# The first modulation of a two-layer diffusion trunk: sixteen weight blocks split over TensorE, VectorE and GpSimd, or all on TensorE with 128-column passes

## The chip, the cores and the metric

One core of one Trainium2 chip. The metric is device microseconds (us) of one execution of the whole kernel, which is one launch. The median of three runs of the kernel before is 2028.92 us (2028.03 to 2032.21).

## The reference, cut to what matters

Two layers of a transformer trunk over 512 latent tokens and 256 context tokens of width 1024. Each layer begins with a modulated RMS norm, followed by one wide input projection:

```python
silu_c = jax.nn.silu(c)          # latent condition, (1, 1024)
silu_cc = jax.nn.silu(c_ctx)     # context condition, (1024,)
for l in range(DEPTH):
    mod = silu_c @ w_mod[l] + b_mod[l]       # 6 * 1024 columns
    mod_c = silu_cc @ w_mod[l] + b_mod[l]
    sh1, sc1, g1, sh2, sc2, g2 = jnp.split(mod[:, None, :], 6, axis=-1)
    csh1, csc1, cg1, csh2, csc2, cg2 = jnp.split(mod_c, 6)
    h = rms_norm(x, norm1[l]) * (1 + sc1) + sh1
    hc = rms_norm(ctx, norm1[l]) * (1 + csc1) + csh1
    ... = jnp.split(h @ w_in[l], IN_SPLITS, axis=-1)
    # two attention branches, gates, output projection, SwiGLU
```

The "first modulation" is the part of this that must be done before anything else in layer 0 can be: the shift `sh1` and the scale `sc1` for both conditions. They take 2048 columns of `w_mod[0]`, which are 16 blocks of 128 columns (8 of shift, numbers 0 to 7, and 8 of scale, numbers 8 to 15), each 128 x 1024 in f32 and 512 KB.

## The kernel before, in words

Channels lie on partitions: x is eight tiles of 128 channels by 768 tokens (512 latent, 256 context), numbered k = 0 to 7. A product with a weight is done in three passes of reduced f32 (`fp32r`): both operands are split into a high and a low half (`h` and `hl` of the activations, `wh` and `wl` of a weight), and high by high, high by low and low by high are summed in PSUM.

`start` (L532 on) is the opening of the program, until the first three projections `gk`, `gv` and `gq` stand in PSUM. Its steps, with the names that the profile uses:

- `token` (L565) loads an x tile; `square` (L569, ACT) and `total` (L573, DVE) sum the squares; `means` (L576, tile `st`, PE) averages over channels; `eps` and `power` (POOL) form the inverse root; `widen` (L591, tile `rb`, PE) spreads it over the partitions; `normed` (L599, DVE) multiplies each x tile by it.
- The modulation of one block n. There are three ways, picked by a letter in the table `FIRST`. **p**: `product` (L606) does eight matmuls on PE with the weight block as the stationary operand and the two columns of `ccol` (the two conditions) as the moving one; the result is 128 x 2. **d**: `reduced` (L613) multiplies and sums on DVE twice, once for each condition, along the rows of a transposed block (`wmodT`). **g**: the latent condition on DVE in this way, the context condition by a multiply on POOL (`times`, L617) and a sum on ACT (`summed`, L620). The ways d and g need the conditions as rows on all partitions (`crow`), made by 16 matmuls (`spread`, L549) and four copies (`unspread`, L557). Five blocks go by p, three by d, eight by g.
- `settle` (L623, DVE) adds the bias, and for a scale block multiplies by the norm's gain (tiles `mod` and `A`).
- `modulate` (L632) applies scale and shift to x tile k: it needs blocks k and 8 + k. Then `high` (L640, ACT) and `low` (L644, POOL or DVE) make `h` and `hl`. The strings `HOWU` and `HOWL` say which engine modulates and which makes the low half, tile by tile.
- `wraw`, `whigh`, `wlow` load and split the three projection weights (`wr`, `wh`, `wl`).
- `multiply` (L664, tile `pj`) does the three passes for projection i, token group s (512 latent, then 256 context) and tile k, and `evac` hands a finished PSUM tile to the next stage.

The order on every engine in this opening is set by `Ops.run` (L275): a list scheduler with a fixed cost for each step, which writes out one order for all engines. `FIRST` is the order of the loads on the SP queue ("x" an x tile, "w" a projection weight, a number a block). Into the gaps that the scheduler foresees on PE it puts `idle` matmuls (L723), 128 x 128 products with the identity whose result nobody reads, at a density of `WARM` = 0.8. Buffers of loaded blocks are reused: the load of a block waits for the users of the block five before it.

Everything behind the opening is scheduled by the same code in both kernels.

Of the kernel before, what the change touches and what calls it, by code (L numbers as in the profile page):

```python
# [12 lines left out]
F32 = mybir.dt.float32  # L13
F32R = mybir.dt.float32r
AF = mybir.ActivationFunctionType
ALU = mybir.AluOpType
# [4 lines left out]
P = 128  # L21
D = 1024
KB = D // P
# [21 lines left out]
for _n in ORDER:  # L45
    for _j in range(COLS[_n][1]):
# [28 lines left out]
]  # L75


FIRST = "x x x x 10p x x x x 0g 8d 1g 13p w 9p w 2p 11g 12p 3d w 4g 5g 6g 14d 7d 15g"

HOWU, HOWL, HOWW = "aaavaaav", "ggvggvgv", "ggv"  # L80
START, HOP, LAND = 4.06, 0.15, 0.25
SAME = dict(v=0.22, a=0.0, g=0.0, p=0.0)
WARM = 0.8
PROD = 2.5


RATE = dict(a=(0.06, 0.00083, "a"), e=(0.28, 0.00083, "a"), v=(0.065, 0.00105, "v"), w=(0.065, 0.00058, "v"),
            g=(0.07, 0.00218, "g"), p=(0.0, 0.19, "g"))
# [175 lines left out]
class Ops:  # L264
# [60 lines left out]
class Trunk:  # L325
# [206 lines left out]
    def start(self, h, pool, others):  # L532


        nc, d = self.nc, self.d
        mod = self.mod[0]
        spans = ((0, S), (S, T))
        nt = T // P
        row = lambda n, count: [pool.tile([P, D], F32, tag="row", name=self.name(n)) for _ in range(count)]
        crow, junk = row("crow", 2), row("junk", 3)  # L540
# [8 lines left out]
        def spread(i):  # L549
            cp = tiles["cp", i] = self.ps("n", "cp")  # L550
            for j in range(4):
                c = 2 * (4 * (i % 2) + j) + i // 2
                nc.tensor.matmul(
                    cp[:, j * P : (j + 1) * P], self.ccol[:, c : c + 1].to_broadcast([P, P]), self.ident,
                    start=True, stop=True)

        def unspread(i):  # L557
            half = i % 2
            nc.scalar.activation(crow[i // 2][:, half * 512 : half * 512 + 512], tiles["cp", i], AF.Copy)

        rows = []
        for i in range(4):
            rows.append(add("a", 0.48, unspread, (i,), [add("p", (1.71, 1.71, 0.87, 0.87)[i], spread, (i,), [], 0)], 0))

        def token(k):  # L565
            x.append(self.slot("x"))
# [36 lines left out]
        def fetch(n, src):  # L603
            raws[n] = self.raw(src, pool=pool)

        def product(n, i):  # L606
            m = self.bank(tiles, i)[:, 2 * n : 2 * n + 2]
            for j in range(KB):
                nc.tensor.matmul(
                    m, raws[n][:, j * P : (j + 1) * P], self.ccol[:, 2 * j : 2 * j + 2],  # L610
                    start=(j == 0), stop=(j == KB - 1), skip_group_check=True)

        def reduced(n, s):  # L613
            nc.vector.tensor_tensor_reduce(
                junk[0], raws[n], crow[s], 1.0, 0.0, ALU.mult, ALU.add, mod[:, s, n : n + 1])

        def times(n, to):  # L617
            nc.gpsimd.tensor_tensor(to, raws[n], crow[1], op=ALU.mult)

        def summed(n, to):  # L620
            nc.scalar.activation(to, to, AF.Copy, accum_out=mod[:, 1, n : n + 1])

        def settle(n, i):  # L623
            m = mod[:, :, n] if i is None else self.bank(tiles, i)[:, 2 * n : 2 * n + 2]
            if n < KB:
                nc.vector.tensor_scalar(mod[:, :, n], m, more[:, n : n + 1], None, op0=ALU.add)
            else:
                k = n - KB
                nc.vector.tensor_scalar(
                    self.A[0][0][:, :, k], m, more[:, n : n + 1], self.norms[:, 0, k : k + 1], op0=ALU.add, op1=ALU.mult)  # L630
# [7 lines left out]
                nc.vector.tensor_scalar(u, u, scale, shift, op0=ALU.mult, op1=ALU.add)  # L638

        def high(k):  # L640
            h[0].append(self.slot("h", F32R))
            nc.scalar.activation(h[0][k], x[k], AF.Copy)

        def low(k, eng):  # L644
            h[1].append(self.slot("hl", F32R))
            (nc.gpsimd if eng == "g" else nc.vector).tensor_tensor(
                h[1][k], x[k], h[0][k][:].bitcast(F32), op=ALU.subtract)

# [24 lines left out]
        def evac(i):  # L673
            reach(others[i])

        loaded, got, free, wdone, sums = [], {}, [], [], []
        products = 0
        last = None
        for what in FIRST.split():
            if what == "x":  # L680
                k = len(loaded)
                loaded.append(add("d", 1.09, token, (k,), [], 1))
                sq = add("a", 0.74, square, (k,), [loaded[k]], 1)
                last = add("v", 0.87, total, (k,), [last, sq], 1) if k else sq
                if k < KB - 1:
                    continue
                last = add("v", 0.08, eps, (), [add("p", 1.28, means, (), [last], 0)], 0)
                early = [
                    add("p", c, widen, (s,), [add("g", g, power, (s,), [last], 0)], 0)
                    for s, c, g in ((0, 0.86, 0.96), (1, 0.43, 0.63))]  # L690
                ready = [
                    [add("v", c, normed, (k, s), [early[s], loaded[k]], 2) for s, c in ((0, 0.6), (1, 0.33))]
                    for k in range(KB)]
            elif what == "w":
                i = len(wdone)
                hi = add("a", 0.95, whigh, (i,), [add("d", 1.45, wraw, (i,), [], 1)], 3)
                eng = HOWW[i]
                wdone.append((hi, add(eng, 2.31 if eng == "g" else 1.13, wlow, (i, eng), [hi], 3)))
            else:
                n, how = int(what[:-1]), what[-1]  # L700
                src = d["wmod0"][products] if how == "p" else d["wmodT"][n]
                at = add("d", 1.45, fetch, (n, src), free[-5] if len(free) >= 5 else [], 1)
                which = None
                if how == "p":
                    which = products
                    products += 1
                    users = ends = [add("p", PROD, product, (n, which), [at], 3)]
                else:
                    users = [add("v", 1.14, reduced, (n, s), [at] + rows, 3) for s in range(1 + (how == "d"))]
                    ends = users  # L710
                    if how == "g":
                        to = junk[1 + len(sums) % 2]
                        users = users + [add("g", 2.31, times, (n, to), [at] + rows + sums[-2:-1], 3)]
                        sums.append(add("a", 1.04, summed, (n, to), users[-1:], 3))
                        ends = ends + sums[-1:]
                free.append(users)
                got[n] = add("v", 0.16, settle, (n, which), ends, 1)
# [1070 lines left out]
    def run(self):  # L1788
        nc, tc, d = self.nc, self.tc, self.d
        joint = [(0, S), (S, T)]  # L1790
        self.flow = None
        with (
# [9 lines left out]
            h = ([], [])  # L1802
            with (
                tc.tile_pool(name="ps0n", bufs=1, space=PSUM, reuse_waits="tile") as psn,
                tc.tile_pool(name="ps0", bufs=1, space=PSUM, reuse_waits="tile") as psa,
                tc.tile_pool(name="n0", bufs=1, reuse_waits="tile") as pool_,
            ):
                self.psum = dict(n=psn, a=psa)
                pool = _Bufs(pool_, dict(rs=1, row=5, more=1, wr=5), dict(qt=self.spool))
                self.constants(cpool)  # L1810
                at = Front()
                spare = _Bufs(None, {}, dict(qt=self.spool))
                todo = self.prologue(0, h, joint, spare, at)
                self.start(h, pool, todo)
            xd = [self.dpool.tile([P, S], F32, name=f"xd{k}") for k in range(KB)]
            for l in range(DEPTH):
# [3 lines left out]
                n = spans[-1][1]  # L1820
# [3 lines left out]
                with (  # L1824
# [7 lines left out]
                    if not last:  # L1832
                        crow = self.conditions(stack.enter_context(
                            tc.tile_pool(name=f"c{l}", bufs=1, reuse_waits="tile")))
                        one = lambda l, n: lambda: self.mod_one(l, n, crow)
                        beside = [one(0, n) for n in range(16, 44)]
                    with tc.tile_pool(name=f"m{l}", bufs=1, reuse_waits="tile") as pool_:
                        pool = _Bufs(pool_, dict(rs=2, qt=5), slots)
# [4 lines left out]
                        x = []  # L1843
# [22 lines left out]
                    h = ([], [])  # L1866
# [27 lines left out]
                    if not last:  # L1894
                        at = Front()
# [126 lines left out]
def _layout(a):  # L2022

    c = np.ascontiguousarray
# [4 lines left out]
    def blocks(m):  # L2029

        k, n = m.shape
        return m.reshape(k // P, P, n // P, P).transpose(2, 1, 0, 3).reshape(n // P, P, k)

    win = []
    for l in range(DEPTH):
# [18 lines left out]
        wmod0=blocks(wm[0][:, : 2 * D])[[int(w[:-1]) for w in FIRST.split() if w[-1] == "p"]],  # L2054
# [26 lines left out]
```

## Time and profile before

| | |
|---|---|
| median of three runs | 2028.92 us (2028.03 to 2032.21) |
| the profiled execution | 2031.42 us, of which the profile's span is 2029.6 us |
| mean granted TensorE clock | 0.977 |
| PE busy in the span | 1954.4 us (96%) |
| DVE, ACT, POOL busy | 1373.0, 884.9, 532.4 us |
| last matmul of the opening (L671) starts | 84.29 us |

The profile shows one execution. A row of the timeline gives a start, a duration, an engine, the line, the operation, and output and inputs by name. A plain f32 matmul leaves two rows on PE, and two rows of weight load on PEld; an `fp32r` matmul leaves one of each. A table of windows gives for each stretch, after its start and end, its length, then the busy time and number of rows of each engine, the clock granted to TensorE as a share of full speed, the busy share of the DMA engines, and GB/s. Matmuls are pipelined, so the distance between starts, and not the duration of one row, is what a matmul costs in a stream.

### The profile page before, as it was taken

How to read it: one execution, taken by the hardware profiler on the slowest of the kernel's cores; microseconds unless marked ns; L12 is line 12 of the kernel's file. 1: busy time of each engine (PE TensorE's matmuls, PEld its weight loads, DVE VectorE, ACT ScalarE, POOL GpSimd, SP SyncE). 2: the span in 40 equal slices, each digit the busy share in tenths (PEclk: the TensorE clock that was granted, in tenths of full speed). 3: DMA queues.
4: the chain of work that ended last, by engine and by line, in shares of the span. 5: the costliest groups of instructions: out<-in, count | busy, mean ns of one | idle time of the engine just before them, and what ended most of it. 6: DMA issues, size and time to landing. Idle time of an engine off the chain costs nothing. (4 is left out here: it accounts for less than half of the span.)

```text
span 2029.6 us, 29667 instructions
## 1 busy us (share of the span) xinstructions
PE 1954.4 (96%) x11468; PEld 1767.9 (87%) x11468; DVE 1373.0 (68%) x2470; ACT 884.9 (44%) x1640; POOL 532.4 (26%) x273
## 2 busy tenths in 40 slices
PE   7999999989999999999999979999999989999998
PEld 6888999977899999999899868889988988888887
DVE  7577888766987999888857576888643563232326
ACT  4466666542235543333424245666543442222224
POOL 6522222234300000000000134332345124435444
PEclk7899999989999999999999989999999989999999
DMA  7211122134563134456321322112223632323233
GB/s 285 70 56 42 37 60 79 58 117 133 182 240 123 60 123 142 144 177 215 118 73 52 103 95 63 51 52 63 76 86 112 197 95 87 113 82 112 75 122 94
DMA packets 74364, 216.50 MB, mean 107 GB/s; under 512 B 8560, under 2 KB 12784, under 8 KB 74224
## 3 DMA queue, kind: packets, MB, share of 16 engines
q1 hardware_dynamic: 74224, 214.61, 33.0%
q8 instruction: 90, 1.47, 0.3%
q14 instruction: 50, 0.41, 0.1%
HBM read 202.52 MB, written 6.82 MB: 103 GB/s over the span
## 5 line engine op out<-in xcount | busy, mean ns | idle before, releaser
L359 POOL TENSOR_TENSOR wl<-wr,wh 128x1024 fp32r<-128x1024 f32 (+2 forms) x177 | 388.6, 2200 | 1159.7 <-ACT wh L357 1152.5
L357 ACT ACTIVATE wh<-wr 128x1024 fp32r<-128x1024 f32 (+2 forms) x253 | 231.7, 917 | 568.4 <-issue 188.8
L372 PE MATMUL pj<-h,wh 128*128 128x512 f32 (+1 forms) x720 | 265.3, 372 | 8.5 <-ACT wh L357 4.4
L372 PE MATMUL pj<-hl,wh 128*128 128x512 f32 (+1 forms) x720 | 257.4, 358 | 3.1 <-DVE hl L528 3.1
L372 PE MATMUL pj<-h,wl 128*128 128x512 f32 (+1 forms) x720 | 256.5, 357 | 0.6 <-POOL wl L359 0.5
L372 PE MATMUL po<-ph,wh 128*128 128x512 f32 (+1 forms) x560 | 192.6, 345 | 0.0
L372 PE MATMUL po<-pl,wh 128*128 128x512 f32 (+1 forms) x560 | 192.5, 345 | 0.0
L372 PE MATMUL po<-ph,wl 128*128 128x512 f32 (+1 forms) x560 | 191.3, 345 | 0.0
L1577 PE MATMUL qu<-r,w 128*128 128x384 f32 x960 | 177.3, 337 | 5.7 <-ACT tt L1584 3.1
L1444 DVE SCALAR_TENSOR_TENSOR x<-po,G,x 128x256 f32<-128x256 f32 (+3 forms) x176 | 101.2, 589 | 120.5 <-PE po L372 120.3
L1577 PEld LDWEIGHTS qu<-r,w 128*128 128x128 f32 x960 | 167.5, 189 | 9.4 <-ACT tt L1584 6.2
L372 PEld LDWEIGHTS pj<-h,wh 128*128 128x128 f32 x720 | 139.4, 194 | 25.1 <-ACT wh L357 4.9
L372 PEld LDWEIGHTS pj<-h,wl 128*128 128x128 f32 x720 | 138.9, 193 | 21.0 <-POOL wl L359 1.5
L372 PEld LDWEIGHTS pj<-hl,wh 128*128 128x128 f32 x720 | 139.8, 194 | 19.2 <-DVE hl L528 4.0
L372 PE MATMUL pf<-hl,wh 128*128 128x512 f32 (+1 forms) x384 | 144.0, 375 | 2.2 <-DVE hl L528 2.1
L372 PE MATMUL pf<-h,wh 128*128 128x512 f32 (+1 forms) x384 | 144.0, 375 | 0.9 <-ACT h L527 0.9
L372 PE MATMUL pf<-h,wl 128*128 128x512 f32 (+1 forms) x384 | 143.4, 373 | 0.0
L1004 ACT ACTIVATE pth<-tp 128x512 fp32r<-128x512 f32 x176 | 103.5, 595 | 67.5 <-PE tp L1054 37.5
L1005 DVE TENSOR_TENSOR ptl<-tp,pth 128x512 fp32r<-128x512 f32 x176 | 119.7, 685 | 14.9 <-ACT pth L1004 13.2
L1469 ACT ACTIVATE w<-wr 128x512 fp32r<-128x512 f32 x120 | 73.7, 628 | 103.3 <-PE qv L1577 22.1
L372 PEld LDWEIGHTS po<-pl,wh 128*128 128x128 f32 x560 | 105.6, 189 | 13.2
L372 PEld LDWEIGHTS po<-ph,wl 128*128 128x128 f32 x560 | 104.9, 188 | 13.7
(243 smaller groups left out, 4436.6 us busy)
## 6 DMA issues: line engine op xcount, KB each, us to landing
wr<-wmodT SPq DMA_DIRECT2D x91, 512.0 KB, 3.8
wr<-wfi SPq DMA_DIRECT2D x88, 512.0 KB, 3.5
wr<-win SPq DMA_DIRECT2D x68, 512.0 KB, 3.5
wr<-wo SPq DMA_DIRECT2D x32, 512.0 KB, 4.1
wr<-wfo SPq DMA_DIRECT2D x40, 256.0 KB, 2.7
wr<-wfo SPq DMA_DIRECT2D x24, 384.0 KB, 3.0
wr<-wp SPq DMA_DIRECT2D x32, 256.0 KB, 3.1
x<-x SPq DMA_DIRECT2D x16, 384.0 KB, 7.7
```

Source lines behind the costliest of these rows:

```text
L357: nc.scalar.activation(hi, raw, AF.Copy)
L359: (eng or nc.gpsimd).tensor_tensor(lo, raw, hi[:].bitcast(F32), op=ALU.subtract)
L372: nc.tensor.matmul(ps[:, : b - a], u[:, c], v[k][:, a:b], start=(k == 0 and i == 0), stop=(k == nk - 1 and i == 2),)
L1004: nc.scalar.activation(hi, tp, AF.Copy)
L1005: nc.vector.tensor_tensor(lo, tp, hi[:].bitcast(F32), op=ALU.subtract)
L1444: self.nc.vector.scalar_tensor_tensor(x[j][:, f:u], ps[:, f - a : u - a], self.G[l][i][:, s, j : j + 1], x[j][:, f:u], op0=ALU.mult, op1=A ...
L1469: nc.scalar.activation(t[:, :n], src, AF.Copy)
L1577: nc.tensor.matmul(banks[bank], u[:, c], v, start=(first and k == 0 and i == 0), stop=(k == kn - 1 and i == 2), skip_group_check=True)
```

## The change

The ways d and g go, with `crow`, `spread`, `unspread`, `reduced`, `times` and `summed`. All sixteen blocks go through `product`, and each of its eight matmuls has 128 moving columns now instead of two: the same two columns of `ccol` repeated 64 times by a stride of zero. All 128 output columns of a block lie side by side in a PSUM bank; `settle` reads the first two. Two PSUM banks (`mp`) are used in turn, four blocks to a bank, before as after. A new constant `AHEAD` = 10 gives ten buffers of blocks instead of five (the five row buffers go), `FIRST` has another order of loads, `HOWU` and `HOWL` alternate the engines, the scheduler's cost of a product is 1.8 instead of 2.5, and the 16 tiles of h and hl are taken at the start of the opening.

```diff
-FIRST = "x x x x 10p x x x x 0g 8d 1g 13p w 9p w 2p 11g 12p 3d w 4g 5g 6g 14d 7d 15g"
-HOWU, HOWL, HOWW = "aaavaaav", "ggvggvgv", "ggv"
+FIRST = "8 x x 0 x x 9 x x 1 x x 10 2 w 11 3 w 12 4 w 13 5 14 6 15 7"
+AHEAD = 10
+HOWU, HOWL, HOWW = "avavavav", "gvgvgvgv", "ggv"
...
-PROD = 2.5
+PROD = 1.8
...
+        for k in range(KB):
+            h[0].append(self.slot("h", F32R))
+            h[1].append(self.slot("hl", F32R))
...
+        def moved(i):
+            return self.bank(tiles, i)[:, i // 2 % 4 * P : i // 2 % 4 * P + P]
+
         def product(n, i):
-            m = self.bank(tiles, i)[:, 2 * n : 2 * n + 2]
             for j in range(KB):
                 nc.tensor.matmul(
-                    m, raws[n][:, j * P : (j + 1) * P], self.ccol[:, 2 * j : 2 * j + 2],
+                    moved(i).rearrange("p (a b) -> p a b", b=2), raws[n][:, j * P : (j + 1) * P],
+                    self.ccol[:, 2 * j : 2 * j + 2].unsqueeze(1).to_broadcast([P, P // 2, 2]),
                     start=(j == 0), stop=(j == KB - 1), skip_group_check=True)
...
         def settle(n, i):
-            m = mod[:, :, n] if i is None else self.bank(tiles, i)[:, 2 * n : 2 * n + 2]
+            m = moved(i)[:, 0:2]
...
-                n, how = int(what[:-1]), what[-1]
...
+                n, i = int(what), len(free)
+                at = add("d", 1.45, fetch, (n, d["wmod0"][i]), free[-AHEAD] if i >= AHEAD else [], 1)
+                free.append([add("p", PROD, product, (n, i), [at], 3)])
+                got[n] = add("v", 0.16, settle, (n, i), free[-1], 1)
...
-                pool = _Bufs(pool_, dict(rs=1, row=5, more=1, wr=5), dict(qt=self.spool))
+                pool = _Bufs(pool_, dict(rs=1, more=1, wr=AHEAD), dict(qt=self.spool))
```

The lines of the changed file are numbered differently: `product` is L598, `means` L565, `widen` L581, `settle` L606 and L609, `modulate` on DVE L618, `high` L621, `low` L624, `wlow` L639, `multiply` L649 and `idle` L686.

On PE, the part of the opening between the average over channels (`st`) and the first passes of the projections (`pj`) reads so in the kernel before, where the projections' passes stand between the products (`mp`):

```order
L579 MATMUL st_226<-ones,sq_140 128x1 x6
L723 MATMUL idle_122<-ident_sb 128x128 x8
L595 MATMUL rb_253<-ident_sb,rs_243 128x128 x4
L595 MATMUL rb_262<-ident_sb,rs_243 128x128 x2
L609 MATMUL mp_177<-ccol_sb,wr_241 128x2 x8
L609 MATMUL mp_176<-ccol_sb,wr_275 128x2 x8
L609 MATMUL mp_177<-ccol_sb,wr_302 128x2 x8
L671 MATMUL pj_339<-h_298,wh_277 128x512
L671 MATMUL pj_339<-hl_307,wh_277 128x512
L671 MATMUL pj_339<-h_298,wl_285 128x512
L609 MATMUL mp_176<-ccol_sb,wr_329 128x2 x8
```

The same place on PE in the changed kernel, from `st` on:

```order
L565 MATMUL st_267<-ones,sq_160 128x1 x6
L598 MATMUL mp_149<-ccol_sb,wr_255 128x128 x8
L581 MATMUL rb_293<-ident_sb,rs_287 128x128 x4
L581 MATMUL rb_303<-ident_sb,rs_287 128x128 x2
L598 MATMUL mp_148<-ccol_sb,wr_275 128x128 x8
L598 MATMUL mp_149<-ccol_sb,wr_290 128x128 x8
L598 MATMUL mp_148<-ccol_sb,wr_318 128x128 x8
L598 MATMUL mp_149<-ccol_sb,wr_332 128x128 x8
L598 MATMUL mp_148<-ccol_sb,wr_359 128x128 x8
```

Five more products follow there without a break, and only behind the sixteenth does the first pass of a projection stand; the 144 passes then come one projection after the other.

On DVE, the changed kernel has these rows from the last `normed` to the second low half made there; the rows on `A` and `mod` are `settle`, and they stand between the modulations (x), the low half of a projection weight (`wl`) and those of the activations (`hl`):

```order
L606 TENSOR_SCALAR mod_104<-mp_149,more_114 128x2
L618 TENSOR_SCALAR x_158<-x_158,A_0_106,mod_104 128x512
L618 TENSOR_SCALAR x_158<-x_158,A_0_106,mod_104 128x256
L618 TENSOR_SCALAR x_184<-x_184,A_0_106,mod_104 128x512
L618 TENSOR_SCALAR x_184<-x_184,A_0_106,mod_104 128x256
L609 TENSOR_SCALAR A_0_106<-mp_148,more_114,norms_sb 128x2
L639 TENSOR_TENSOR wl_410<-wr_341,wh_370 128x1024
L624 TENSOR_TENSOR hl_120<-x_158,h_119 128x768
L606 TENSOR_SCALAR mod_104<-mp_149,more_114 128x2
L624 TENSOR_TENSOR hl_124<-x_184,h_123 128x768
```

In the kernel before the 15 long reductions of L614 stood among such rows. A product writes the PSUM bank that the `settle` two blocks earlier reads, and waits for that `settle`.

On the SP queue the eight x tiles stood ahead of nearly all blocks; in the changed kernel the loads behind the constants begin so, with four blocks among the x tiles:

```order
L351 DMA wr_139<-wmod 128x1024
L553 DMA x_146<-x 128x768
L553 DMA x_158<-x 128x768
L351 DMA wr_162<-wmod 128x1024
L553 DMA x_174<-x 128x768
L553 DMA x_184<-x 128x768
L351 DMA wr_188<-wmod 128x1024
L553 DMA x_201<-x 128x768
L553 DMA x_211<-x 128x768
L351 DMA wr_215<-wmod 128x1024
L553 DMA x_228<-x 128x768
L553 DMA x_238<-x 128x768
```

So x tile 7 is the twelfth large load instead of the ninth. Behind the opening all engines have the same instructions in the same order in both kernels.

More of the change, by code (lines that the diff above doesn't have):

```diff
@@ L538, in start @@
         nt = T // P
-        row = lambda n, count: [pool.tile([P, D], F32, tag="row", name=self.name(n)) for _ in range(count)]
-        crow, junk = row("crow", 2), row("junk", 3)
         more = pool.tile([P, 16], F32, tag="more", name=self.name("more"))
@@ L545, in start @@
         tiles, x, sqs, rb, raws = {}, [], [], {}, {}
+        for k in range(KB):
+            h[0].append(self.slot("h", F32R))
+            h[1].append(self.slot("hl", F32R))
         todo = Ops()
         add = todo.add
[L549 to L563, printed above, removed]
         def token(k):
@@ L640, in high @@
         def high(k):
-            h[0].append(self.slot("h", F32R))
             nc.scalar.activation(h[0][k], x[k], AF.Copy)
         def low(k, eng):
-            h[1].append(self.slot("hl", F32R))
             (nc.gpsimd if eng == "g" else nc.vector).tensor_tensor(
@@ L674, in evac @@
             reach(others[i])
-        loaded, got, free, wdone, sums = [], {}, [], [], []
-        products = 0
+        loaded, got, free, wdone = [], {}, [], []
         last = None
@@ L699, in start @@
             else:
-                n, how = int(what[:-1]), what[-1]
[L701 to L717, printed above, removed]
+                n, i = int(what), len(free)
+                at = add("d", 1.45, fetch, (n, d["wmod0"][i]), free[-AHEAD] if i >= AHEAD else [], 1)
+                free.append([add("p", PROD, product, (n, i), [at], 3)])
+                got[n] = add("v", 0.16, settle, (n, i), free[-1], 1)
         for t, n in ((self.cos, "cos"), (self.sin, "sin")):
@@ L2053, in _layout @@
         gain=np.concatenate([two(a["q_gain"]), two(a["k_gain"])]).T,
-        wmod0=blocks(wm[0][:, : 2 * D])[[int(w[:-1]) for w in FIRST.split() if w[-1] == "p"]],
+        wmod0=blocks(wm[0][:, : 2 * D])[[int(w) for w in FIRST.split() if w.isdigit()]],
         wmodT=wmt.reshape(DEPTH * 48, P, D),
```

7 lines of the change are left out of this document (removed).

## The prediction

> **What bounds the kernel now.** I read the page first: how busy PE is, over the whole span.
>
> ```profile
> span 2029.6 us, 29667 instructions
> PE 1954.4 (96%) x11468; PEld 1767.9 (87%) x11468; DVE 1373.0 (68%) x2470; ACT 884.9 (44%) x1640; POOL 532.4 (26%) x273
> ```
>
> PE is busy for 96%, so time can be won only where it idles or its clock is low. Then the table of windows over the opening, in steps of 4 us, and one window behind it (after the bounds and the length: PE, PEld, DVE, ACT, POOL busy, granted clock, DMA share, GB/s).
>
> ```profile
> 36.00:40.00 4.00, 3.89 (x13) 3.01 (x13) 3.96 (x5) 2.34 (x4) 4.00 (x2) 0.50 1.03 417
> 44.00:48.00 4.00, 0.85 (x4) 0.37 (x2) 4.00 (x3) 1.15 (x2) 4.00 (x3) 0.94 0.35 119
> 60.00:64.00 4.00, 1.68 (x8) 1.06 (x6) 3.96 (x6) 0.38 (x1) 2.35 (x1) 1.00 0.00 0
> 64.00:68.00 4.00, 1.68 (x3) 1.08 (x4) 4.00 (x9) 3.94 (x7) 0.05 (x1) 0.57 0.00 0
> 76.00:80.00 4.00, 4.00 (x36) 4.00 (x35) 1.58 (x4) 2.43 (x6) 1.87 (x2) 1.00 0.03 6
> 84.30:200.00 115.70, 113.87 (x783) 104.56 (x782) 81.03 (x171) 67.84 (x135) 36.06 (x17) 1.00 0.19 60
> ```
>
> Up to about 72 us PE idles by turns and has half its clock by turns, while DVE is full in every window from 36 to 68 us. At 76 us PE is full, and from 84.3 us on it stays so (113.87 of 115.70 us). So the opening is bound by something other than PE, and its end pushes all that follows. The waits of the first 90 us say by what:
>
> ```profile
> ACT x L636 <- DVE mod L626: 5.3, 1, 5.3
> PE pj L671 <- ACT h L642: 4.2, 1, 4.2
> PE pj L671 <- DVE wl L661: 4.1, 1, 4.1
> ```
>
> PE waits for the halves of x and of a weight; these wait for the modulation, and that for `mod`, which DVE makes with its reductions. The timeline shows the end of that chain: the last low half, passes of the projections, the last of them, and the first work behind them.
>
> ```profile
> 71.86 0.96 DVE L646 TENSOR_TENSOR hl<-x,h 128x768 fp32r<-128x768 f32 x1 [0.91 <-ACT h L642]
> ...
> 73.77 0.40 PE L671 MATMUL pj<-hl,wh 128*128 128x512 f32 x1
> ...
> 75.40 0.40 PE L671 MATMUL pj<-h,wl 128*128 128x512 f32 x1
> ...
> 84.29 0.28 PE L671 MATMUL pj<-h,wl 128*128 128x256 f32 x1
> 84.41 1.40 PE L797 MATMUL st<-hones,sq 128*128 128x2 f32 x12
> ```
>
> The opening ends at 84.4 us. Its 512-column passes follow each other at 0.233 us (73.77 to 75.40 is seven steps), the 256-column ones at 0.12 us.
>
> **What goes.** The reductions:
>
> ```profile
> L614 DVE CUSTOM_DVE_ANT_0 junk<-wr,crow 128x1024 f32<-128x1024 f32 x15 | 29.1, 1941 | 0.2
> L618 POOL TENSOR_TENSOR junk<-wr,crow 128x1024 f32<-128x1024 f32 x7 | 21.9, 3150 | 16.8 <-DMA wr<-wmodT 16.8
> ```
>
> That is 29.1 us of DVE and 21.9 us of POOL, in an opening of 84 us in which DVE is the engine that is late. With them go the ACT sums and the `crow` work. What is late next has to be found by walking through the new order.
>
> **The price of a wide product.** No row shows a moving operand that repeats two columns. The nearest are the idle matmuls, also plain f32, 128 x 128 with 128 columns, at half and at full clock; then the narrow products; then PE with narrow products somewhat later.
>
> ```profile
> 14.10:20.20 6.10, 6.01 (x28) 6.08 (x28) 0.50 1.03 412
> 54.50:57.20 2.70, 2.70 (x27) 2.70 (x26) 1.00 0.82 305
> ...
> 26.20:30.60 4.40, 4.37 (x40) 4.40 (x40) 0.98 0.46 157
> ...
> 30.70:32.50 1.80, 1.80 (x10) 1.80 (x10) 1.80 (x3) 0.17 (x1) 1.80 (x2) 0.50 0.99 357
> ```
>
> An idle row costs 0.100 us at full clock (27 in 2.70) and 0.215 at half; a narrow row 0.109 (40 in 4.37). Each matmul leaves two rows, and PEld is as full as PE, so the loading of the 128 x 128 block sets the pace and the 64-fold stream hides under it. A product of eight matmuls is 16 rows: I take 1.7 us, bounds 1.6 and 2.0 (the 16 idle rows at 21.51 us took 2.03 with their tail). The last row has a second meaning: after 4 us in which PE was full of narrow products the clock fell to 0.50. Idle matmuls of 128 columns brought it up in the windows above. So I expect full clock through the wide products; at half clock one would cost 16 x 0.215 = 3.4 us.
>
> The Trainium skill, "TensorE: Matmul & The Clock Gate", Back-to-back issue gap, gives about 81 ns for a sustained pair of weight load and 128-column matmul. By it, as an estimate, a product would be 16 x 0.081 = 1.3 us. This trace has 0.100 at best, so the sum keeps 1.7.
>
> **When the loads land.** The windows give the bytes, the page the sizes, and the first product before the delay of a landing:
>
> ```profile
> wr<-wmodT SPq DMA_DIRECT2D x91, 512.0 KB, 3.8
> ...
> x<-x SPq DMA_DIRECT2D x16, 384.0 KB, 7.7
> ```
>
> ```profile
> 4.00:8.00 4.00, 4.00 (x27) 4.00 (x26) 0.17 (x1) 2.25 (x4) 0.00 (x0) 1.00 0.88 281
> 8.00:12.00 4.00, 1.85 (x17) 1.68 (x16) 1.92 (x2) 2.83 (x6) 0.00 (x0) 1.00 0.94 365
> 12.00:16.00 4.00, 3.99 (x24) 4.00 (x25) 3.09 (x5) 2.95 (x5) 0.00 (x0) 0.67 1.04 416
> 16.00:20.00 4.00, 4.00 (x21) 4.00 (x20) 3.90 (x3) 0.65 (x1) 2.78 (x1) 0.50 1.03 410
> 20.00:24.00 4.00, 3.54 (x31) 3.35 (x30) 3.97 (x9) 2.21 (x3) 1.48 (x2) 0.98 1.03 408
> ```
>
> ```profile
> 12.01 2.32 PE L609 MATMUL mp<-ccol_sb,wr 128*128 128x2 f32 x16 [2.16 <-DMA wr<-wmod]
> ...
> 20.25 1.40 PE L579 MATMUL st<-ones,sq 128*128 128x1 f32 x12
> ...
> 24.72 1.67 PE L595 MATMUL rb<-ident_sb,rs 128*128 128x128 f32 x12 [1.18 <-POOL rs L589]
> ```
>
> With 0.14 MB of constants by 4 us, 1.27 MB have passed by 8, 2.73 by 12, 4.39 by 16, 6.03 by 20 and 7.66 by 24 us, then 0.41 MB each us while SP isn't held up; ten buffers mean that it isn't. Before, the first block was the fifth load (2.24 MB, passed at 10.7 us) and was used at 12.0: a landing comes 1.3 us behind its bytes. In the new order the first block lands at 7.2 us, x tile 7 (5.38 MB) at 19.7, the fifth block (5.91 MB) at 21.0, the last (13.8 MB, with four projection weights) at 40.2. Moving blocks ahead of x thus delays x by about 4 us, and that counts.
>
> **The sum.** The fifth product runs from 21.0 to 22.7 us; the squares are summed by then (19.7 + 0.84 + 0.96 = 21.5). `st` starts at 22.7 instead of 20.25; `rb` starts 4.47 us after `st`, as before, at 27.2 (the sixth product hides in that wait), and ends at 28.9. Now PE is the late one: ten products without a break, 17.0 us, to 45.9; each block has landed well before. DVE must keep up, since a product waits for the `settle` two blocks earlier, and these stand in DVE's row behind `wl` and `hl`. Those can be long:
>
> ```profile
> 38.00 13.19 POOL L618 TENSOR_TENSOR junk<-wr,crow 128x1024 f32<-128x1024 f32 x4
> ...
> 39.05 3.16 DVE L646 TENSOR_TENSOR hl<-x,h 128x768 fp32r<-128x768 f32 x1
> ```
>
> Beside POOL's work a low half took 3.16 us on DVE, alone 0.96 (the row at 71.86): 2.2 us more. POOL has three long operations left there (`wl` and two `hl`), so bounds are none and 6.6 us; most DVE work there has slack of about one, so I take one: 48.1 us. The last x tile doesn't add: settle, modulation, high and low half:
>
> ```profile
> 70.08 0.87 DVE L638 TENSOR_SCALAR x<-x,A,mod 128x512 f32<-128x512 f32 x2
> 70.98 0.85 ACT L642 ACTIVATE h<-x 128x768 fp32r<-128x768 f32 x1 [2.07 <-DVE x L638]
> ```
>
> With the low half's 0.96 and some 0.5 for settle and hops that is 3.2 us, and PE needs 21 passes (4.9 us) before it asks for tile 7. Then all 144 passes: 72 x 0.233 + 72 x 0.12 = 25.4, to 73.5 us. Against 84.4 that is **10.9 us earlier**, and PE stays full behind, so the end moves by as much. The profiled execution took 2031.4 us, so 2020.5; from the median of the runs, 2.5 us lower, 2018.0. I take 2019.3.
>
> The other edits I cost at nothing: h tiles taken early (16 + 8 x + 8 squares are 32 of 45 slots); the other engines for modulation and low halves, covered by that DVE slack (one more lock, 2.2 us, if it is gone); the bias columns, constants and bytes are the same.
>
> **The rivals.** (a) *DVE and POOL block each other more*, all three times: 6.6 instead of 2.2 us, end at 77.9, 2024.9. For it speak the long rows above; against it, POOL has 7 operations less.
> (b) *The wide products are slow*, the one that ends on the other side: either PE reads the repeated pair slower than the identity, or the gate doesn't count such passes and halves the clock. A product at 3.4 us makes PE late from the first landing: 7.2 us + 24 idle matmuls 5.1 + `st` and `rb` 3.1 + 16 x 3.4 + 25.4 = 95.2, which is 10.8 later: 2042.2. It decides from 40.8 + 16 p = 84.4, so p = 2.7 us, 0.17 us a row. For it: no row shows this operand, and clocks of 0.50 are common here. Against it: the idle rows, equal in shape.
> (c) *The loads set the end*: if products outrun the blocks, the last lands at 40.2, and 40.2 + 1.7 + 2.2 + 25.4 = 69.5, 14.9 earlier: 2016.5, or 2014.0 from the median. By the Trainium skill's pair of 81 ns, named above, this is where it would go. Against it: no row under 0.100.
> (d) *The shift is given back*: a later wait that doesn't move with the opening absorbs it, 2029. Against it: PE full behind 84.3 us, and nothing there is reordered.
>
> **How the numbers follow.** Forecast 0.67, (a) 0.12, (b) 0.13, (c) 0.04, (d) 0.04. About 0.2% (4 us) is what a measurement of this kernel can tell from no change. Forecast and (c) are faster, (a) lies at the edge, which I split: faster 0.77, same 0.10, slower 0.13. The range: product price and locks at their low bounds win 1.0 + 2.2 more, 2028.9 - 14.1 = 2014.8; all locks give 2024.9. That holds forecast, (c) and about half of (a).
>
> **What would show it.** In the new profile: the first work behind the opening (`st` with `hones`) at 73 to 74 us; clock 1.00 from 28 to 73 us (right) or 0.50 (b); 16 product rows in 1.7 us; ten products back to back behind `rb` at 27 us, or PE waiting for DVE's `settle` between them (a); the last block landing near 40 us. Wrong it would be above all if a product row costs more than 0.17 us.

## The result, and the profile after

The changed kernel takes **2016.82 us** (median of 4 runs, 2013.23 to 2017.97), beside 2029.05 us of the kernel before (4 runs, 2028.03 to 2032.21): a ratio of 0.9934, 95% interval 0.9917 to 0.9951. That is 12.2 us faster; 2019.3 was forecast, in a range of 2014.8 to 2024.9. The profiled execution took 2017.36 us at a mean clock of 0.987 (0.977 before).

The page of the profile after, its span and its first part:

```profile
span 2015.6 us, 29828 instructions
PE 1950.2 (97%) x11580; PEld 1767.1 (88%) x11580; DVE 1342.3 (67%) x2445; ACT 872.5 (43%) x1618; POOL 505.0 (25%) x265
```

Over the whole span nearly nothing shows: DVE has 31 us less and POOL 27, PE 4 us less. (The 15 reductions and the 7 multiplies of POOL that went belong to four blocks that went by d and seven by g, as the table `FIRST` has it; the description of the kernel says three and eight.) One window over the opening says more. First the kernel before, then the kernel after (bounds, length, busy time and rows of PE, PEld, DVE, ACT, POOL, then granted clock, DMA share, GB/s):

```profile
0.00:72.00 72.00, 54.97 (x287) 48.87 (x288) 59.55 (x88) 35.11 (x51) 41.01 (x20) 0.79 0.60 221
```

```profile
0.00:72.00 72.00, 67.04 (x486) 63.59 (x487) 31.63 (x67) 28.75 (x39) 20.10 (x15) 1.00 0.59 223
```

PE is busy for 12 us more of these 72, DVE for 28 us less, and the clock is 1.00 instead of 0.79. In windows of 4 us, after; all but the second are places that the prediction shows of before:

```profile
36.00:40.00 4.00, 4.00 (x38) 4.00 (x37) 4.00 (x7) 3.52 (x5) 0.93 (x2) 1.00 1.02 402
40.00:44.00 4.00, 2.98 (x24) 2.60 (x23) 4.00 (x7) 0.02 (x1) 2.17 (x1) 1.00 1.00 393
44.00:48.00 4.00, 4.00 (x35) 3.91 (x34) 1.68 (x5) 2.86 (x4) 1.03 (x1) 1.00 0.10 38
60.00:64.00 4.00, 4.00 (x21) 3.34 (x20) 0.00 (x0) 0.10 (x1) 0.00 (x0) 1.00 0.00 0
64.00:68.00 4.00, 4.00 (x35) 4.00 (x35) 1.66 (x4) 2.37 (x5) 1.91 (x2) 1.00 0.00 0
```

DVE is idle at 60 us, where it was full before; PE is full from 24 us on, with one gap between 40 and 44. The timeline of the kernel after shows what fills it (rows chosen from PE, POOL and DVE: start, duration, engine, line; a group of x16 rows is one product of eight matmuls, and its duration holds the tail of the last row, so that the distance between starts is shorter):

```profile
11.26 1.95 PE L598 MATMUL mp<-ccol_sb,wr 128*128 128x128 f32 x16
13.05 1.50 PE L686 MATMUL idle<-ident_sb 128*128 128x128 f32 x12
...
21.59 2.02 PE L598 MATMUL mp<-ccol_sb,wr 128*128 128x128 f32 x16 [0.54 <-DMA wr<-wmod]
23.45 1.40 PE L565 MATMUL st<-ones,sq 128*128 128x1 f32 x12
24.70 2.03 PE L598 MATMUL mp<-ccol_sb,wr 128*128 128x128 f32 x16
25.12 1.69 POOL L575 TENSOR_TENSOR rs<-rs,expo 128x4 f32<-128x4 f32 x2 [24.68 <-DVE rs L570]
26.57 1.50 PE L581 MATMUL rb<-ident_sb,rs 128*128 128x128 f32 x12
27.91 14.83 PE L598 MATMUL mp<-ccol_sb,wr 128*128 128x128 f32 x128
...
40.00 2.17 POOL L624 TENSOR_TENSOR hl<-x,h 128x768 fp32r<-128x768 f32 x1 [3.07 <-ACT h L621]
40.55 2.42 DVE L624 TENSOR_TENSOR hl<-x,h 128x768 fp32r<-128x768 f32 x1
...
43.36 0.27 DVE L609 TENSOR_SCALAR A<-mp,more,norms_sb 128x2 f32<-128x2 f32 x1
43.68 3.84 PE L598 MATMUL mp<-ccol_sb,wr 128*128 128x128 f32 x32 [0.94 <-DVE A L609]
47.27 0.48 PE L649 MATMUL pj<-h,wh 128*128 128x512 f32 x1
...
72.33 1.40 PE L760 MATMUL st<-hones,sq 128*128 128x2 f32 x12
```

A wide product of 16 rows takes 13.05 - 11.26 = 1.79 us. Ten of them run behind `rb`, with one wait for `settle` (the 0.94 us at 43.68), which stood on DVE behind a low half that took 2.42 us, beside one on POOL (40.00 to 42.17). The projections begin at 47.27, and the first work behind the opening starts at 72.33 instead of 84.41: **12.08 us earlier**.

### The profile page after: what moved, and what is told of

Its sections match the earlier page's. It is cut to its first block, busy times and chain, and to the rows that moved or that the text cites. A ratio compares the mean times of both kernels' runs of the same rounds, so it can differ in the third digit from the quotient of the medians.

```text
span 2015.6 us, 29828 instructions
## 1 busy us (share of the span) xinstructions
PE 1950.2 (97%) x11580; PEld 1767.1 (88%) x11580; DVE 1342.3 (67%) x2445; ACT 872.5 (43%) x1618; POOL 505.0 (25%) x265
## 5 line engine op out<-in xcount | busy, mean ns | idle before, releaser
L1540 PEld LDWEIGHTS qu<-r,w 128*128 128x128 f32 x960 | 166.4, 188 | 12.7 <-ACT tt L1547 9.5
```

What stands on the lines that cost most here:

```text
L1540: nc.tensor.matmul(banks[bank], u[:, c], v, start=(first and k == 0 and i == 0), stop=(k == kn - 1 and i == 2), skip_group_check=True)
```

## The experiments

Theory: the change gains because all reductions leave DVE, and because PE can take them at 1.8 us a product, which it can only while the 128 repeated columns keep its clock at 1.00. Rivals: the columns are an ornament, since the loading of the block sets the pace anyway; the idle matmuls keep the clock; the width alone brings the gain. In all that follows, "the end of the opening" is the start of `st` with `hones`, 84.41 us before and 72.33 after.

### The width: 2, 32 and 64 columns

The changed kernel, with the moving operand of a product cut (here to two columns; for 32 and 64 the pair is repeated 16 and 32 times):

```diff
-                    moved(i).rearrange("p (a b) -> p a b", b=2), raws[n][:, j * P : (j + 1) * P],
-                    self.ccol[:, 2 * j : 2 * j + 2].unsqueeze(1).to_broadcast([P, P // 2, 2]),
+                    moved(i)[:, 0:2], raws[n][:, j * P : (j + 1) * P],
+                    self.ccol[:, 2 * j : 2 * j + 2],
```

> The changed kernel with two moving columns a matmul instead of 128; all else, the order on every engine too, as changed. My theory: the loading of the block sets the pace of a product, and the 64-fold stream keeps the clock. Then two columns cost the same as long as the clock stays, but it won't: from the tenth product on the granted clock falls to 0.50, a product takes 16 x 0.21 = 3.4 us instead of 1.8, the ten behind rb take some 34 instead of 18 us, the first projection passes are at half clock as well, and the whole is 15 to 20 us slower than the changed kernel: about 2034, a little above the kernel before. Rival: the width is without effect and the gain is that of DVE's freed time alone: 2017, clock 1.00 throughout.

> The changed kernel with the two columns repeated 16 times (32 moving columns). If the clock gate follows the share of time in which columns stream through the array, 32 columns are a quarter of what 128 are and the clock falls as with two: 2030 or more, granted clock 0.50 between 28 and 47 us. Rival: any stream above some small width is enough: 2017, clock 1.00. Either way a row at full clock stays at 0.11 us, since loading the block sets the pace.

> The changed kernel with 64 columns a product instead of 128. If the clock follows how much of the array's time is spent streaming (theory), there is a width at which it turns, somewhere above the 32 columns that let it fall to 0.50. A 64-column pair streams 64 rows of the 0.112 us that a row takes at full clock, about half of what the 128-column pair streams. By a smooth rule it lies between the two: clock 0.50 in part of 24 to 66 us, the first wide pass between 50 and 62 us, time 2018 to 2032. By a rule with a threshold it is one or the other: first pass at 47 us and 2015 to 2019, or at 63 us and 2032 to 2038. Rival (the width as such is nothing, the profiles of 2 and 32 columns fell by chance): first pass at 47 us with no window under 0.95.

| columns | median us | ratio to before, 95% | end of the opening, us |
|---|---|---|---|
| 2 | 2038.95 | 1.0040 (1.0024 to 1.0055) | 89.39 |
| 32 | 2035.73 | 1.0035 (1.0022 to 1.0048) | 89.97 |
| 64 | 2020.12 (2 runs) | 0.9948 (0.9929 to 0.9968) | 78.38 |
| 128 (the change) | 2016.82 | 0.9934 (0.9917 to 0.9951) | 72.33 |

With two columns, a window and the timeline:

```profile
36.00:40.00 4.00, 4.00 (x21) 4.00 (x20) 2.06 (x6) 0.45 (x1) 2.78 (x2) 0.50 1.03 401
```

```profile
14.25 1.92 PE L598 MATMUL mp<-ccol_sb,wr 128*128 128x2 f32 x16
...
28.99 34.13 PE L598 MATMUL mp<-ccol_sb,wr 128*128 128x2 f32 x160
62.98 0.77 PE L649 MATMUL pj<-h,wh 128*128 128x512 f32 x1
```

Early on a narrow product takes as long as a wide one (1.92 us with its tail). From about 25 us the clock is 0.50, the ten products take 34.13 us, 3.4 each, and the opening ends 17 us later than with 128 columns and 5 us later than before the change. By medians it is 22 us behind the changed kernel, where 15 to 20 were expected, and 9 us behind the kernel before in its own set (2029.78); what the opening does not account for, some 4 us, is not explained. With 32 columns it is the same:

```profile
36.00:40.00 4.00, 4.00 (x21) 4.00 (x20) 1.48 (x5) 1.18 (x2) 3.50 (x2) 0.50 1.03 400
```

PE and PEld are full in both windows, 4.00 of 4.00 us, and yet the clock is down: what holds it is not how busy the rows look. The Trainium skill, "TensorE: Matmul & The Clock Gate", Part 1, section "What's actually happening", says that the gate is set by how busy PE has been recently; these two windows show that busy time as the profile counts it is not the measure. With 64 columns the clock falls only in part: it is 0.50 from about 25 to 29 us, and from 46 to 56 us, behind the wait for `settle`. The first pass comes at 50.85 us, between the 47.27 of 128 columns and the 62.98 of two:

```profile
24.00:28.00 4.00, 4.00 (x27) 4.00 (x27) 0.39 (x2) 0.72 (x1) 3.24 (x3) 0.68 1.03 410
32.00:36.00 4.00, 4.00 (x38) 4.00 (x38) 4.00 (x11) 3.77 (x5) 3.75 (x3) 1.00 1.03 405
48.00:52.00 4.00, 4.00 (x18) 3.81 (x18) 0.84 (x3) 0.10 (x1) 1.80 (x1) 0.50 0.00 0
```

So the columns do nothing for the pace of a product at full clock, and the clock hangs on them. The rival by which they are an ornament falls. Between 32 and 128 the effect is graded in what it costs (17.6, 6.1, 0 us at the end of the opening); whether a lone window turns at a threshold these runs don't tell.

### The width alone

The kernel before, with the products of its five p blocks 128 columns wide and all else as it was:

```diff
-            m = self.bank(tiles, i)[:, 2 * n : 2 * n + 2]
+            m = self.bank(tiles, i)[:, i // 2 * P : i // 2 * P + P].rearrange("p (a b) -> p a b", b=2)
...
-                    m, raws[n][:, j * P : (j + 1) * P], self.ccol[:, 2 * j : 2 * j + 2],
+                    m, raws[n][:, j * P : (j + 1) * P], self.ccol[:, 2 * j : 2 * j + 2].unsqueeze(1).to_broadcast([P, P // 2, 2]),
...
```

> The kernel before with one part of the change alone: the five products that it has get 128 moving columns; the reductions on DVE and POOL stay. My theory: DVE is what is late in that opening, so a clock that stays up in the stretch from 30 to 41 us only makes PE wait longer for DVE: within 3 us of the kernel before (2026 to 2030). Rival: the clock was the cause of the loss: 8 to 12 us faster (2017 to 2021).

Measured: 2031.14 us, ratio 1.0005 (0.9994 to 1.0015). Two windows of it:

```profile
32.00:36.00 4.00, 3.76 (x31) 3.29 (x30) 4.00 (x8) 0.84 (x2) 2.31 (x2) 1.00 0.91 352
48.00:52.00 4.00, 0.82 (x2) 0.72 (x3) 4.00 (x2) 0.00 (x0) 4.00 (x2) 0.83 0.40 131
```

The clock is 1.00 where it was 0.50, and nothing is won, since DVE is full and PE has nothing to do (0.82 of 4 us at 48). The opening even ends 2.65 us later than before, at 87.06; in this execution the clock was 0.50 from 20 to 28 us, where it was 0.98 and 1.00 before, and whether that is the cause was not tried. With the first experiment this splits the change: **all of the change but the width costs 5 us of the opening, the width alone gains nothing, both gain 12.**

### The idle matmuls

The changed kernel with `WARM = 0.0`, once by itself and once beside the changed kernel on the same chip:

```diff
-WARM = 0.8
+WARM = 0.0
```

> The changed kernel without the idle matmuls. My theory: the wide products keep the clock by themselves: at half clock one takes 3.5 us, longer than the 3.2 us between two blocks, so PE is full and the clock rises within the first two or three products; then 1.8 in 3.2 us is enough to hold it. Within 2 us of the changed kernel (2015 to 2019). Rival: the idle matmuls hold the clock in the first 28 us; without them it is low until the ten products behind rb have run for some microseconds, two or three of these and the fifth cost 3.5 us: 5 to 7 us slower, 2022 to 2024.

> The changed kernel itself, timed beside the same program without its idle matmuls on the same chip. Expected by everybody: 2014 to 2018 us, ratio 0.991 to 0.995 to the kernel before; the grouped-key statistics product at 72.3 us.

> The changed kernel without idle matmuls, timed beside it. Theory (the idle products cost only what stands ahead of the first statistics product, 0.6 us, and the wide products keep the clock by themselves): 0 to 1.5 us faster than the changed kernel, statistics product of the first key projection at 71.7 us. Rival (the 3 us between their medians is real and comes from somewhere behind the opening): 2 to 4 us faster, with the shift growing behind 100 us.

Without them 2013.55 (ratio 0.9916, 0.9901 to 0.9931) in the first and 2016.06 (0.9924, 0.9911 to 0.9938) in the second set; the changed kernel beside the second took 2016.50 (0.9928, 0.9913 to 0.9942). The timeline of the second:

```profile
7.00 3.76 PE L598 MATMUL mp<-ccol_sb,wr 128*128 128x128 f32 x16 [7.00 <-DMA wr<-wmod]
11.11 2.35 PE L598 MATMUL mp<-ccol_sb,wr 128*128 128x128 f32 x16 [0.35 <-DMA wr<-wmod]
14.43 2.02 PE L598 MATMUL mp<-ccol_sb,wr 128*128 128x128 f32 x16 [0.97 <-DMA wr<-wmod]
...
46.58 0.48 PE L649 MATMUL pj<-h,wh 128*128 128x512 f32 x1
```

Only the first two products are slow, which PE makes good while it waits for loads; the opening ends at 71.65 us (72.49 beside it). Wide products keep the clock alone, and the idle matmuls cost 0.6 to 0.8 us. The 3 us between the medians of the first comparisons did not come again beside each other (0.4 us).

The two executions of the *same* changed kernel also show where runs differ: spans of 2015.6 and 2018.4 us with openings that end at 72.33 and 72.49. 2.6 of the 2.8 us arise behind the opening, in stretches that have low clock in every run, as here (after, then the same kernel again):

```profile
1170.00:1215.00 45.00, 35.46 (x170) 30.04 (x170) 25.73 (x51) 20.42 (x41) 12.40 (x7) 0.77 0.14 46
```

```profile
1170.00:1215.00 45.00, 33.01 (x144) 27.90 (x145) 26.00 (x45) 17.89 (x35) 10.10 (x6) 0.73 0.11 36
```

So differences of 1 or 2 us are read below at the end of the opening, which repeats within 0.2 us, and not from medians.

### The buffers

The change also raises the buffers of the blocks from five to ten. Here they are five:

```diff
-AHEAD = 10
+AHEAD = 5
```

> The changed kernel with five buffers for the modulation blocks, as before the change, instead of ten. Theory (loads end near 40 us, 7 us ahead of the last product, and a buffer is free once its product has run; with five, block n waits for product n-5): the loads come later by up to the time of five products, 9 us, but the last block still comes ahead of its product or at most 2 us behind, key statistics at 72 to 74 us, total within 2 us of the changed kernel. Rival (the depth of the loads is what makes the ten products run on end): pauses ahead of the products from 30 us on, clock below 1.00, statistics at 76 us or later.

Measured: 2019.33 us (3 runs, ratio 0.9946, 0.9929 to 0.9964), end of the opening 72.71 us. Two pauses, one of them new:

```profile
37.63 5.60 PE L598 MATMUL mp<-ccol_sb,wr 128*128 128x128 f32 x48 [0.26 <-DVE x L618]
44.05 3.84 PE L598 MATMUL mp<-ccol_sb,wr 128*128 128x128 f32 x32 [0.82 <-DVE A L609]
```

The opening ends 0.38 us later than with ten buffers, but the depth is not the cause: 0.36 us of that are there at `st` already, which waits for no block behind the fifth, and so for none that takes a used buffer:

```profile
23.81 1.40 PE L565 MATMUL st<-ones,sq 128*128 128x1 f32 x12
```

From the end of `rb` to the first pass it is 19.37 us with five buffers (28.27 to 47.64) and 19.36 with ten: the new pause is made good by a shorter second one. So the depth is worth nothing that this run shows, and the 2.5 us between the medians are no larger than the difference just shown between two executions of one kernel.

### What is left: the wait for `settle`, and the order of the loads

A product may run only two ahead of its `settle`, because there are two accumulator banks. Three banks, on top of no idle matmuls (the bank of the idle matmuls goes, and `st` and the second `rb` share one, to make room; `...` stands for these edits):

```diff
-            return self.bank(tiles, i)[:, i // 2 % 4 * P : i // 2 % 4 * P + P]
+            return self.bank(tiles, i)[:, i // 3 % 4 * P : i // 3 % 4 * P + P]
...
-            tiles["banks"] = [self.ps("n", "mp") for _ in range(2)]
-        return tiles["banks"][i % 2]
+            tiles["banks"] = [self.ps("n", "mp") for _ in range(3)]
+        return tiles["banks"][i % 3]
```

> The kernel without idle matmuls, with three accumulator banks for the products instead of two (the statistics and the second row broadcast share a bank to make room), so that a product waits for the addition of the product three before it. Theory (the 0.94 us that TensorE waits for the addition near 42 us is the price of the one block of VectorE and GpSimd, and it reaches the end because a product may run only two ahead): that wait is gone, the first wide pass at 45.6 us instead of 46.6, the key statistics at 70.7 instead of 71.7, the total about 1 us lower, which the medians cannot tell. Rival (the wait only takes its place at the last additions or at the first low half, which VectorE delivers late anyway): first wide pass at 46.5 and statistics at 71.6 as before.

```profile
26.93 18.03 PE L599 MATMUL mp<-ccol_sb,wr 128*128 128x128 f32 x160
...
39.57 2.43 DVE L625 TENSOR_TENSOR hl<-x,h 128x768 fp32r<-128x768 f32 x1
...
44.72 0.48 PE L650 MATMUL pj<-h,wh 128*128 128x512 f32 x1
```

The long low half is still there (2.43 us), but PE no longer waits: ten products in 17.79 us (26.93 to 44.72), against 27.91 to 47.27 = 19.36 after (and 19.37 without idle matmuls). So this block of DVE beside POOL, which the prediction calls a lock, cost the changed kernel 1.57 us. The opening ends at **69.78 us**, the earliest of all: 1.9 us ahead of the kernel without idle matmuls, its nearest relative, and 2.5 us ahead of the changed kernel; 2014.99 us, ratio 0.9922 (0.9906 to 0.9938). I had expected 70.7: I had counted only the wait of 0.94 that the profile names.

Then the loads: before `st` PE has only five products, though it has time for more. Blocks and activations alternate, with two banks, and a middle way with three, both without idle matmuls:

```diff
-FIRST = "8 x x 0 x x 9 x x 1 x x 10 2 w 11 3 w 12 4 w 13 5 14 6 15 7"
+FIRST = "8 x 0 x 9 x 1 x 10 x 2 x 11 x 3 x 12 4 w 13 5 w 14 6 w 15 7"
```

```diff
-FIRST = "8 x x 0 x x 9 x x 1 x x 10 2 w 11 3 w 12 4 w 13 5 14 6 15 7"
+FIRST = "8 x 0 x 9 x x 1 x x 10 x 2 x 11 w 3 12 w 4 13 w 5 14 6 15 7"
```

> The kernel without idle matmuls, with the loads of the modulation blocks laid alternately with the activations (one block, one activation, and so on) instead of one block to two activations, so that TensorE has a product in each 2.2 us and nine of the sixteen are done ahead of the statistics instead of five. Theory (with the products at 1.8 us each and the clock at 1.00, TensorE is idle about half of the first 21 us only because of the order of the loads): statistics product at about 26.7 us instead of 22.8, the row broadcast at 30, six products behind it, the first wide pass at 44 to 45.5 us instead of 46.7, bounded then by VectorE and GpSimd and no more by the products, the key statistics at 69 to 70.5 us instead of 71.7, time 1 to 2.5 us below the kernel without idle matmuls. Rival (VectorE's chain from the row broadcast sets the end of the opening, so a later broadcast makes it later by the same): the first wide pass at 48 to 50 us, 1 to 4 us slower.

> The same with three banks, and with six modulation blocks loaded ahead of the last activation instead of five, against eight in the alternating order. Theory (in the alternating order VectorE's chain of some 16 us from the row broadcast became the bound, with pauses in the passes and a lower clock; here the broadcast comes at 29 to 30 us and 16 us later is 45 to 46): first wide pass at 44 to 45 us without pauses over 0.5 us, no window under 0.95 from 40 to 72 us, key statistics at 69.3 to 70.7. Rival (VectorE bounds already): pauses at 44 to 48 us, clock below 0.9 there, statistics at 71 to 73.

The alternating order has its first projection pass at 43.77 instead of 46.58, but then PE waits for what DVE makes:

```profile
43.77 0.48 PE L649 MATMUL pj<-h,wh 128*128 128x512 f32 x1
...
45.48 0.49 PE L649 MATMUL pj<-h,wh 128*128 128x512 f32 x1 [0.77 <-ACT h L621]
46.90 0.50 PE L649 MATMUL pj<-hl,wh 128*128 128x512 f32 x1 [0.92 <-DVE hl L624]
```

```profile
48.00:52.00 4.00, 4.00 (x13) 3.19 (x12) 4.00 (x5) 1.63 (x2) 1.47 (x1) 0.66 0.00 0
```

DVE is full, PE waits, and the clock is 0.66 behind that: the opening ends at 72.69, a loss of 1.0 against 71.65. The first pass came earlier, as the theory had it; the end came later by 1 us, through VectorE, as the rival had it. Its median, 2012.26 (ratio 0.9913, 0.9900 to 0.9926), is not explained by that. `st` came at 28.66 us, 2 us later than the theory had it. The middle way (2012.00, ratio 0.9919, 0.9902 to 0.9935) went as its theory had it: first pass at 44.33, the end at 70.71, the clock at 1.00 throughout; its passes pause twice for DVE's low halves, for 0.34 and 0.30 us by the waits. Neither beats the plain order with three banks at the end of the opening. By the medians all these versions overlap (the middle way has the lowest, with a later opening than three banks alone; why is not shown); against the kernel before, each is clearly faster.

## Why the prediction was right

The time, 2016.8 instead of 2019.3, lies in the range, and the mechanism was the predicted one. Of the 2.5 us between the two, 1.2 are the opening; the rest is the starting point, which was taken between the profiled execution and the median of before (from the median the forecast is 2018.0). Step by step, in us of the profile:

| step | predicted | measured |
|---|---|---|
| fifth product starts | 21.0 | 21.59 |
| `st` starts | 22.7 | 23.45 |
| `rb` starts | 27.2 (4.47 behind `st`) | 26.57 (3.12 behind) |
| a wide product | 1.7 | 1.79 |
| ten products and the lock, from the end of `rb` | 17.0 + 2.2 = 19.2 | 19.36 (17.79 of it with three banks, so 1.57 for the lock) |
| last block lands | 40.2 | about 40.8 (issued at 30.48, 10.3 to landing) |
| projections begin | 48.1 | 47.27 |
| 144 passes | 25.4 | 25.06 |
| end of the opening | 73.5 | 72.33 |

- **The pace and the clock.** Right: 1.00 in every window of 4 us from 24 to 72, and 1.79 us, inside the bounds of 1.6 to 2.0. The reason given, that columns of the kind that the idle matmuls had would hold the clock, is shown by the three widths.
- **The term mis-sized most** is the wait from `st` to `rb`, carried over from before as 4.47 us. Before, POOL's two powers began 2.44 us behind `st` and took 2.94 us (the last row below); after, with the reductions of the modulation gone from both engines, they began 1.67 us behind it and took 1.69: 3.12 in all. That is 1.35 us too much in the sum. The rows show where the late beginning came from: `rs`, which the powers wait for, stood on DVE right behind a reduction and began 2.20 us behind `st`; in the changed kernel it was 1.43. The powers took 2.94 us in both kernels with reductions beside them (before, and before with wide products) and 1.68 or 1.69 us in all eleven without; so it goes with the reductions, but how these slow the powers was not tried.

```profile
21.30 1.22 DVE L614 CUSTOM_DVE_ANT_0 junk<-wr,crow 128x1024 f32<-128x1024 f32 x1
...
22.45 0.16 DVE L584 TENSOR_SCALAR rs<-st 128x6 f32<-128x6 f32 x1
...
22.69 2.94 POOL L589 TENSOR_TENSOR rs<-rs,expo 128x4 f32<-128x4 f32 x2 [2.52 <-DVE rs L584]
```

- **The other errors** are smaller: `st` was forecast 0.75 us too early, `rb` and the passes 0.3 to 0.4 too long each, and together with the wait they make the 1.2 us by which the opening ended sooner. That the ten products and the lock came out within 0.2 us is luck in part: the products took 0.8 us more and the lock 0.6 us less than the sum had.
- **The lock.** Taken once, from bounds of none and three: it came once, 1.46 us above the 0.96 of a low half alone instead of 2.2. The prediction counted three long operations of POOL there; five begin between the end of `rb` and the first pass, and only beside the one at 40.00 us did a row of DVE grow long. Rival (a), three times, didn't come. That it reaches the end through the wait for `settle` is shown by the three banks.
- **Rival (b)**, slow products at 3.4 us, didn't come here but is real: two columns gave just that product (34.13 us for ten) and a slower kernel. Its opening ended at 89.39 us and not at 95.2, since the clock fell only at about 25 us and the products ahead of that cost 1.8; the time was 2038.95 instead of 2042.2.
- **Rival (c)**, the loads set the end: no. PE waited for blocks for 0.5 us in all, ahead of the fifth product, and a product row cost 0.112 us, not less than 0.100. By the estimate from the Trainium skill's pair of 81 ns ("TensorE: Matmul & The Clock Gate", Back-to-back issue gap) it would have been 1.3 us a product; the trace disagrees with that for these f32 products.
- **Rival (d)**, the shift is given back: no. Equal instructions are 12.1 us earlier at 90 us, 12.0 at 350 and 11.3 at 1200. Then the shift grows to 12.7 us at 1240 and 14.3 at 1257, and the profiled pair differs by 14.06 us at the end, because before has low clock in two short stretches, near 1227 and near 1247 us, where after has 1.00 at the same work some 12 us earlier. The second of them, before, then after:

```profile
1244.00:1247.00 3.00, 1.95 (x8) 1.71 (x9) 2.88 (x4) 0.00 (x0) 0.64 (x1) 0.76 0.40 153
1247.00:1250.00 3.00, 3.00 (x11) 2.37 (x10) 2.19 (x5) 0.01 (x1) 0.00 (x0) 0.67 0.00 0
```

```profile
1232.00:1235.00 3.00, 2.66 (x14) 2.29 (x15) 2.91 (x5) 0.00 (x0) 0.00 (x0) 1.00 0.20 81
1235.00:1238.00 3.00, 3.00 (x24) 2.88 (x23) 1.99 (x5) 2.32 (x4) 1.19 (x1) 1.00 0.00 0
```

That is scatter of the kind that two runs of one kernel show (the second execution of the changed kernel is 10.6 us ahead of before at 1300 us); the 12.2 us by medians agree with the opening's 12.1.

- **Idle matmuls** were costed as kept and as the thing that warms the clock. That they are no longer needed was not foreseen; it is worth 0.6 to 0.8 us.
- **The other edits** were costed at nothing. Five buffers bear that out for the ten buffers. The early tiles of h and hl and the other engines for modulations and low halves were not undone by themselves, so no run shows what they are worth.

## What to carry to other kernels

When an engine's work is moved to TensorE, price it at the clock that the moved work itself will hold: here the same sixteen blocks cost 1.8 us each with 128 streamed columns and 3.4 with 2 or 32, and the sign of the change hung on it. The wider stream cost nothing here (1.79 us a product with 128 columns, 1.78 with two, at full clock), but it pays only once the engine that was late (here DVE) is relieved too. And a term that is "as before" in a sum has to be read again for what its engine was doing before: the 4.47 us from `st` to `rb` shrank by 1.4 us with the reductions gone.

## What the runs showed of the hardware that was not expected

- A full PE is not a warm PE: with 2 and with 32 columns PE was busy for 4.00 of 4.00 us, and PEld too, at a granted clock of 0.50.
- In the first microseconds the granted clock of the windows does not fit the rows. In the second run without idle matmuls the first product took 3.76 us for 16 rows (the row at 7.00), the price at half clock, while the window that holds its start reads 1.00 (the changed kernel's first product took 3.11 us in one execution and 2.02 in the other, with 1.00 in the windows of both):

```profile
0.00:8.00 8.00, 0.99 (x5) 1.03 (x6) 1.02 (x10) 1.65 (x3) 0.20 (x4) 1.00 0.55 175
8.00:24.00 16.00, 12.27 (x89) 11.49 (x89) 7.62 (x12) 7.27 (x9) 0.00 (x0) 1.00 1.02 404
```

- The second of these windows has PE busy for 77% (12.27 of 16 us), and products every 3.2 us with pauses between, and this was enough for the clock: from the third product on each took 2.02 us with its tail.
